# A hybrid attention and retention block on one core: the halves of retention's queries and keys exchanged by DMA

## The chip, the cores and the metric

The kernel runs on one core of a Trainium2 chip. The metric is the time of one execution in microseconds of device time, lower is better. Before the change the median of three runs is 3148.3 us (3146.62 to 3150.13).

## What is computed

One block of a streaming encoder on 4096 tokens of width 1024, in float32. Cut to what matters here:

```python
u = rms_norm(h, pre_norm_gain)
proj = einsum('bsd,de->bse', u, w_in)                 # 4104 columns
fq, fk, fv, fz, ff, rq, rk, rv, rz = split(proj)
fox = forgetting_attention(fq, fk, fv, ff + bias)     # 8 heads of 64
ret = retention(rq, rk, rv)                           # 4 heads of 128, chunkwise
out = concat([fox * silu(fz), ret * silu(rz)]) @ w_out
return h + rms_norm(out, post_norm_gain)
```

Retention rotates its queries and keys first, and this is where the change sits. The head's 128 rows are two halves of 64:

```python
def rotary(x, pos):
    x1, x2 = x[..., :64], x[..., 64:]
    return concatenate([x1 * cos - x2 * sin, x1 * sin + x2 * cos], axis=-1)
```

## The kernel before

Everything is cut into blocks of 512 tokens, eight of them. Products run on TensorE in three float16 passes. Two streams share the engines. The first is attention (`attention`): for each head and query block it takes key tiles of 128 in turn, computes scores, lets ScalarE write two exponentials, lets GpSimd subtract them (`ptt`, L308), and multiplies with the values. Beside it run the "max tiles" (`max_tile`, L999): one matmul (in the rows `ps<-kc,xq`) and one VectorE reduction (`mrow<-ps`) each, 1152 of them, which find the row maxima of later items. The second stream is the "filler": the projections of the other heads, then the output product. A credit scheme in the program decides how many filler steps are written between two attention steps, so that the order on each engine is fixed when the program is built (`tc.manual_schedule()`), and each engine works through its own list in order. PSUM has eight banks that all products take in turn; a product that needs a bank waits until the work on the bank's last contents is done.

Small follow-up work is written as Python generators. `spawn` starts one, and each `tick` (one per attention step and one per filler step) moves every live generator on to its next `yield`. So a number of `yield`s is a distance in program order, not a time.

The filler's second part, `fill_r`, projects retention's heads, two at a time (`hh` = 0 and 1), in 16 passes (two groups by eight token blocks). Per pass there are four products for queries and keys, in the order query 0, key 0, query 1, key 1. Each gives one 128 x 512 PSUM bank, and `rope_evac` takes it: ScalarE evicts it (L755), then four VectorE operations rotate it. That is 64 rotations in all. `rp` holds the cosine and sine tables of the block. All VectorE `tensor_tensor` operations go through the helper `tt`, so that their line is L141; all matmuls through `mm` (L104), all DMAs are issued by SyncE's queue through `dma` (L107), in one order.

`retention` then does one head and block: it first transposes the rotated keys on TensorE (L811), later multiplies keys with queries, updates the head's running state on VectorE (`states`, four operations `state<-state,s`), and multiplies the queries with the states. It starts at a fixed place (`pump`) while the next projection runs: for `hh` = 0 that is while the product for query 1 runs, directly behind the rotation of key 0.

Of the kernel before, what the change touches and what calls it, by code (L numbers as in the profile page):

```python
# [13 lines left out]
ALU = mybir.AluOpType  # L14
# [18 lines left out]
WAGE = 2  # L33
VAGE = 5
MAGE = 9
LEAD = 12
RAWAGE = 8
SAGE = 4
# [15 lines left out]
def kernel(  # L54
# [33 lines left out]
    def SB(tag, shape, dt=F32):  # L88
        cnt[0] += 1
        slot = SHARED.get(tag, tag)  # L90
        return sbp.tile(shape, dt, tag=slot, name=f"{tag}_{cnt[0]}", bufs=BUFS.get(slot, 1))
# [48 lines left out]
    def tt(o, a, b, op):  # L140
        nc.vector.tensor_tensor(out=o, in0=a, in1=b, op=op)  # L141

    def ts(o, a, s1, s2, op0, op1):
        nc.vector.tensor_scalar(out=o, in0=a, scalar1=s1, scalar2=s2, op0=op0, op1=op1)  # L144
# [130 lines left out]
    def iz(g, part):  # L275
        return gsc[g][part][:, KT : KT + 1]
# [477 lines left out]
    def rope_evac(p, rp, o, key):  # L754
        nc.scalar.activation(out=o, in_=p, func=AF.Copy, scale=iz(key[1], 0))  # L755
        yield 1
        yield 1
        t2 = SB("s2", [128, 512])
        tt(t2[0:64], o[64:128], rp[64:128, 1, :], ALU.mult)
        yield 1  # L760
        tt(t2[64:128], o[0:64], rp[0:64, 1, :], ALU.mult)
        yield 1
        tt(o, o, rp[:, 0, :], ALU.mult)
        yield 1
        tt(o, o, t2, ALU.add)
        done.add(key)
# [108 lines left out]
    def fill_r(G):  # L875
# [4 lines left out]
        for b, X, hook, last in group_blocks(G, tuple(range(NB))):  # L880
            vt = SB("s4", [128, 4, 256])
            zt = SB("s4", [128, 4, 256])
            for t in range(4):
                p = PS()
                for k in G.units(1, unit_N(W[1], X, t, ((0, 512),), [p])):
                    if last and t == 3 and k is not None:
                        nxt.release("wn", k)
                    yield WAIT if k is None else 3 * COST_MM + pump(k)
                spawn(evac_r(g, p, t, vt, zt))
                if t == 2:  # L890
                    rp = SB("s4", [128, 2, 512])
                    dma(rp, rope[b])
            for hh in range(2):
                qk = []
                for j in (hh, 2 + hh):
                    p = PS()
                    for k in G.units(0, unit_T(W[0], X, j * 128, p)):
                        if j == 3 and k is not None:
                            hook(k)
                            if last:  # L900
                                nxt.release("wt", k)
                        yield WAIT if k is None else 3 * COST_MM + pump(k)
                    o = SB("s2", [128, 512])
                    spawn(rope_evac(p, rp, o, ("rope", g, b, j)))
                    qk.append(o)
                rets.append(retention(b, g, hh, qk[0], qk[1], vt, zt))
                fresh[0] = rets[-1]
# [101 lines left out]
    def max_row(n, xq, mrow, qb):  # L1009
# [3 lines left out]
        ts(m4, m4, gsc[items[n][0] // 4][0][:, KT + 5 : KT + 6], None, ALU.add, ALU.bypass)  # L1013
        for _ in range(MAGE):
            yield 1
# [19 lines left out]
    def attention():  # L1035
# [52 lines left out]
        def max_rate(g):  # L1088

            rate = 0.0  # L1090
            for j in range(len(items)):
                if mdue[j] > mdone[0]:
                    if j >= 4 and first_step[j - 4] > g + 16:
                        break
                    rate = max(rate, (mdue[j] - mdone[0]) / max(first_step[j] - LEAD - g, 1))
            return min(2, math.ceil(rate - 1e-9))
# [210 lines left out]
def _constants(S):  # L1307
    import numpy as np

    half = 64  # L1310
    f = np.float32
    inv = (f(1.0) / (f(10000.0) ** (np.arange(half, dtype=f) / f(half)))).astype(f)
    ang = (np.arange(S, dtype=f)[:, None] * inv[None, :]).astype(f)
    cos = np.cos(ang.astype(np.float64)).astype(f).T
    sin = np.sin(ang.astype(np.float64)).astype(f).T
    tab = np.stack([np.concatenate([cos, cos], 0), np.concatenate([sin, -sin], 0)], 0)
    rope = np.ascontiguousarray(tab.reshape(2, 128, S // 512, 512).transpose(2, 1, 0, 3))
    lg = np.log1p(-np.exp(np.linspace(math.log(1.0 / 32), math.log(1.0 / 512), RH)))
    dk = 128.0 ** -0.5
    i = np.arange(128)  # L1320
    ii, jj = i[None, :], i[:, None]
    tri = (jj <= ii).astype(f)
    mT = np.where(jj > ii, f(NEG), f(0.0)).astype(f)
    parts = [tri, np.eye(128, dtype=f)]
    for h in range(RH):
        same = (ii // 64) == (jj // 64)
        earlier = (jj // 64) < (ii // 64)
        dist = np.where(same, np.abs(ii - jj), ii - jj)
        d = np.where(same | earlier, np.exp(lg[h] * dist), 0.0)
        parts.append((d * np.exp(-lg[h] * (ii + 1.0)) * dk).astype(f))  # L1330
    parts.append(np.stack([np.exp(lg[h] * (127.0 - i)) * dk for h in range(RH)], 1).astype(f))
    parts.append(np.stack([GN_EPS * np.exp(-2.0 * lg[h] * (i + 1.0)) for h in range(RH)], 1).astype(f))
    parts += [mT, np.ascontiguousarray(mT.T)]
    cst = np.ascontiguousarray(np.concatenate(parts, 1))
    aux = np.zeros((2 * R1 + CP + 2, 512), np.float16)
    aux[0:CP], aux[CP] = TOP, MID
    aux[2 * R1 : 2 * R1 + CP], aux[2 * R1 + CP], aux[2 * R1 + CP + 1] = TOP, MID, LOW
    return rope, cst, aux, [float(np.exp(lg[h] * 128.0)) for h in range(RH)]
# [26 lines left out]
```

## Time and profile before

| what | value |
|---|---|
| median of three runs | 3148.3 us |
| the profiled execution | 3151.84 us, its span 3150.0 us |
| mean granted TensorE clock | 0.985 |
| busy share of the span: TensorE, VectorE, ScalarE, GpSimd | 96%, 66%, 59%, 43% |
| first and last rotation (start of L755) | 1139.4 and 2704.3 us |

The profiled execution is 0.1% above the median. The span is the time from the first to the last instruction that the profiler recorded. TensorE is busy nearly throughout; its idle stretches are short and mostly end when VectorE finishes something.

### The profile page before, as it was taken

Reading aid. Unit: us, or ns where it says so; the run is one execution under the profiler, and the core shown is the slowest. Engines: PE = TensorE matmul, PEld = TensorE weight load, DVE = VectorE, ACT = ScalarE, POOL = GpSimd, SP = SyncE. Lnnn points to the kernel's source line nnn. Section 1 sums busy time; section 2 is a strip of 40 time slices with the busy share of each in tenths; the row PEclk is TensorE's granted clock in tenths of the full one; section 3 lists DMA queues with packets and bytes.
Section 4 is the critical chain, followed back from the end, with each engine's and each line's share of the span. In section 5 each row is a group of like instructions: output and inputs, shape, how many; then the busy total and the mean of one; then the engine's idle time right before and its main releaser. Section 6 shows DMA issues by size and latency. Waiting matters only on the chain.

```text
span 3150.0 us, 67744 instructions
## 1 busy us (share of the span) xinstructions
PE 3029.2 (96%) x26798; PEld 1794.7 (57%) x26799; DVE 2076.8 (66%) x4372; ACT 1873.1 (59%) x3508; POOL 1351.6 (43%) x1285
## 2 busy tenths in 40 slices
PE   8999989999999999999999999999999999889999
PEld 6666555555555555665555565556556555555554
DVE  6545567446455676777678878776877786645555
ACT  4333345676677667666667675667666766653332
POOL 0000024554555455555545564556455645540000
PEclk9999999999999999999999999999999999999999
DMA  6455753223235231311114223112111321124443
GB/s 179 156 166 152 199 123 95 67 82 93 69 88 134 64 80 35 91 51 52 55 57 101 58 71 97 51 43 78 49 51 45 111 73 33 57 68 141 141 141 120
DMA packets 266174, 284.62 MB, mean 90 GB/s; under 512 B 58976, under 2 KB 212192, under 8 KB 265856
## 3 DMA queue, kind: packets, MB, share of 16 engines
q1 hardware_dynamic: 265856, 280.30, 31.3%
q8 instruction: 210, 3.44, 0.4%
q14 instruction: 108, 0.88, 0.1%
HBM read 194.88 MB, written 88.74 MB: 90 GB/s over the span
## 4 chain that ended last, share of the span: by engine, by line
PE 80%; DVE 12%; ACT 3%; issue 2%; DMA 2%; POOL 1%; SPq 1%; POOLq 0%; DVEq 0%; ACTq 0%
PE ps L104 77%; DVE mrow L999 3%; DVE s L141 2%; DVE s L144 1%; DVE sm L141 1%; DMA rw<-in_w_in_dram 1%; ACT ph L1133 1%; PE ps L1188 1%; ACT pf L1132 1%; SPq L107 1%; PE ps L349 1%; DVE sm L144 1%; DVE s L147 1%; POOL pl L308 1%; POOL sm L308 0%
## 5 line engine op out<-in xcount | busy, mean ns | idle before, releaser
L308 POOL TENSOR_TENSOR pl<-pf,ph 128x512 f16<-128x512 f32 (+3 forms) x1152 | 1281.2, 1117 | 1135.0 <-ACT ph L1133 856.8
L1132 ACT ACTIVATE pf<-ps,gsc 128x512 f32<-128x512 f32 (+3 forms) x1152 | 758.2, 658 | 694.0 <-PE ps L104 677.0
L999 DVE TENSOR_REDUCE mrow<-ps 128x1 f32<-128x512 f32 (+3 forms) x1152 | 717.6, 641 | 356.9 <-PE ps L104 345.8
L104 PE MATMUL ps<-wn,xh 128*128 128x512 f16 (+2 forms) x3840 | 852.7, 359 | 3.1 <-DVE qk L147 2.9
L1133 ACT ACTIVATE ph<-ps,gsc 128x512 f16<-128x512 f32 (+3 forms) x1152 | 754.3, 655 | 0.0
L104 PEld LDWEIGHTS <-xh 128*128 128x128 f16 x4608 | 450.2, 98 | 450.5 <-issue 22.5
L104 PE MATMUL ps<-xh,wt 128*128 128x512 f16 x2688 | 667.7, 381 | 3.4 <-DVE mrow L999 2.0
L104 PEld LDWEIGHTS <-wt 128*128 128x128 f16 x3168 | 308.9, 98 | 356.4 <-issue 24.6
L104 PEld LDWEIGHTS <-ph 128*128 128x128 f16 x8448 | 423.9, 97 | 76.0 <-issue 8.0
L104 PE MATMUL ps<-vt,ph 128*128 128x65 f16 (+1 forms) x8448 | 433.8, 195 | 10.4 <-ACT ph L1133 7.3
L104 PE MATMUL ps<-xq,kc 99*128 99x512 f16 (+3 forms) x1152 | 420.0, 365 | 14.6 <-DMA xq<-MR 9.7
L104 PE MATMUL ps<-vt,pl 128*128 128x65 f16 x4224 | 423.4, 193 | 3.8 <-POOL pl L308 3.8
L104 PE MATMUL ps<-lq,kc 128*128 128x512 f16 (+3 forms) x1152 | 419.1, 364 | 0.0
L104 PE MATMUL ps<-kc,xq 99*128 99x512 f16 (+3 forms) x1152 | 383.1, 364 | 34.3 <-DVE mrow L999 25.1
L104 PEld LDWEIGHTS <-pl 128*128 128x128 f16 x4224 | 393.3, 99 | 5.1 <-POOL pl L308 4.7
L104 PEld LDWEIGHTS <-kc 128*128 128x128 f16 (+1 forms) x3072 | 281.9, 99 | 196.8 <-issue 22.2
L141 DVE TENSOR_TENSOR s<-s,s 64x512 f32<-64x512 f32 (+1 forms) x256 | 258.6, 1010 | 33.3 <-ACT s L755 26.3
L308 POOL TENSOR_TENSOR sm<-sm,nhalf 128x4 f32<-128x4 f32 (+2 forms) x80 | 63.0, 787 | 350.5 <-DVE sm L144 308.5
L104 PEld LDWEIGHTS <-xq 99*128 99x128 f16 x1152 | 112.3, 98 | 139.4 <-issue 9.5
L104 PE MATMUL ps<-wt,xh 128*128 128x512 f16 x768 | 184.0, 381 | 0.0
L141 DVE TENSOR_TENSOR ps<-ps,maskM 128x128 f32<-128x128 f32 x256 | 75.1, 293 | 108.4 <-PE ps L104 107.6
L141 DVE TENSOR_TENSOR xh<-ps,xh 128x256 f16<-128x256 f32 (+1 forms) x128 | 70.3, 555 | 105.5 <-ACT xh L338 86.1
(120 smaller groups left out, 2525.2 us busy)
## 6 DMA issues: line engine op xcount, KB each, us to landing
xh<-XT SPq DMA_DIRECT2D x176, 256.0 KB
rw<-in_w_in_dram SPq DMA_DIRECT2D x104, 256.0 KB
xt<-in_x_dram SPq DMA_DIRECT2D x36, 512.0 KB
s<-MX SPq DMA_DIRECT2D x32, 512.0 KB
out_dram<-xt SPq DMA_DIRECT2D x31, 512.0 KB
s<-in_x_dram SPq DMA_DIRECT2D x28, 512.0 KB
VD<-s SPq DMA_DIRECT2D x16, 516.0 KB
vt<-VD SPq DMA_DIRECT2D x64, 129.0 KB
```

What stands on the lines that cost most here:

```text
L104: nc.tensor.matmul(out=o, lhsT=lhsT, rhs=rhs, start=start, stop=stop, skip_group_check=True)
L107: nc.sync.dma_start(out=o, in_=i)
L141: nc.vector.tensor_tensor(out=o, in0=a, in1=b, op=op)
L144: nc.vector.tensor_scalar(out=o, in0=a, scalar1=s1, scalar2=s2, op0=op0, op1=op1)
L147: nc.vector.scalar_tensor_tensor(out=o, in0=a, scalar=s, in1=b, op0=op0, op1=op1)
L308: nc.gpsimd.tensor_tensor(out=o, in0=a, in1=b, op=op)
L349: nc.tensor.transpose(p[:, t * 128 : (t + 1) * 128], xs[t][:, k * 128 : (k + 1) * 128], idf)
L999: nc.vector.tensor_reduce(out=mrow[:, t, c : c + 1], in_=p[:, 0:w], axis=AX.X, op=ALU.max)
L1132: nc.scalar.activation(out=pf[:, q0:512], in_=st[:, q0:512], func=AF.Exp, scale=es)
L1133: nc.scalar.activation(out=ph[:, q0:512], in_=st[:, q0:512], func=AF.Exp, scale=es)
L1188: nc.tensor.transpose(p[:, e * 128 : (e + 1) * 128], mxt[:, half * 4 + e, :], idf)
```

## The change

The two half products with the sine table, which read one half of the rows and wrote the other, go. Two DMAs within SBUF copy the halves crosswise into `t2`; the cosine product is written directly behind them; six ticks later one VectorE operation multiplies the whole of `t2` with the sine table, and a tick later the addition follows. The sign of the sine rows in the table is exchanged to match.

```diff
+RAGE = 6
@@ rope_evac
         nc.scalar.activation(out=o, in_=p, func=AF.Copy, scale=iz(key[1], 0))
         yield 1
         yield 1
         t2 = SB("s2", [128, 512])
-        tt(t2[0:64], o[64:128], rp[64:128, 1, :], ALU.mult)
-        yield 1
-        tt(t2[64:128], o[0:64], rp[0:64, 1, :], ALU.mult)
-        yield 1
+        dma(t2[0:64], o[64:128])
+        dma(t2[64:128], o[0:64])
         tt(o, o, rp[:, 0, :], ALU.mult)
+        for _ in range(RAGE):
+            yield 1
+        tt(t2, t2, rp[:, 1, :], ALU.mult)
         yield 1
         tt(o, o, t2, ALU.add)
         done.add(key)
@@ _constants
-    tab = np.stack([np.concatenate([cos, cos], 0), np.concatenate([sin, -sin], 0)], 0)
+    tab = np.stack([np.concatenate([cos, cos], 0), np.concatenate([-sin, sin], 0)], 0)
```

The order on TensorE, ScalarE and GpSimd is the same in both programs. VectorE's list has 64 operations fewer, and SyncE's 128 DMAs more.

VectorE's list at one rotation of a key 0 (tile `s2_7243`, with `s2_7251` as `t2` and `s4_7155` as the tables; `mrow` rows are max tiles), before:

```order
L999 TENSOR_REDUCE mrow_7195_36073<-ps_7250_36346 128x1 [waits PE_49]
L141 TENSOR_TENSOR s2_7251_36349<-s2_7243_36330,s4_7155_35852 64x512 [waits Activation_49,Pool_49]
L999 TENSOR_REDUCE mrow_7195_36073<-ps_7255_36362 128x1 [waits PE_49]
L141 TENSOR_TENSOR s2_7251_36349<-s2_7243_36330,s4_7155_35852 64x512
L141 TENSOR_TENSOR s2_7243_36330<-s2_7243_36330,s4_7155_35852 128x512 [waits DMAHW3_49,DVE_49]
L999 TENSOR_REDUCE mrow_7195_36073<-ps_7261_36428 128x1 [waits PE_49]
L141 TENSOR_TENSOR s2_7243_36330<-s2_7243_36330,s2_7251_36349 128x512 [waits DVE_49]
L999 TENSOR_REDUCE mrow_7195_36073<-ps_7265_36449 128x1 [waits PE_49]
```

The same place with the change (line numbers are one or two higher):

```order
L1001 TENSOR_REDUCE mrow_7195_36121<-ps_7250_36395 128x1 [waits PE_49]
L142 TENSOR_TENSOR s2_7243_36379<-s2_7243_36379,s4_7155_35900 128x512 [waits DMAHW1_49,DMAHW0_49,DMAHW3_49,Activation_49,Pool_49]
L1001 TENSOR_REDUCE mrow_7195_36121<-ps_7255_36413 128x1 [waits PE_49]
L1001 TENSOR_REDUCE mrow_7195_36121<-ps_7261_36477 128x1 [waits PE_49]
L142 TENSOR_TENSOR s2_7251_36398<-s2_7251_36398,s4_7155_35900 128x512 [waits Pool_49]
L1001 TENSOR_REDUCE mrow_7195_36121<-ps_7265_36498 128x1 [waits PE_49]
L142 TENSOR_TENSOR s2_7243_36379<-s2_7243_36379,s2_7251_36398 128x512 [waits DVE_49]
```

The cosine product, which writes over `o`, now waits for both DMAs, which read `o`. The addition has moved from ahead of the max tile in bank tile `ps_7265` to behind it.

TensorE's list from that max tile's matmul to the transposes of this key, in both programs the same, here with the change's numbers:

```order
L105 MATMUL ps_7265_36498<-kc_6571_33181,xq_7010_35205 128x512 [waits Activation_49]
L105 LDWEIGHTS wt_5146_26195
L105 MATMUL ps_7244_36381<-xh_6997_35170,wt_5146_26195 128x512
...
L813 MATMUL ps_7266_36505<-csb_1_143,s2_7243_36379 128x128 [waits DVE_49,Activation_49]
L813 MATMUL ps_7266_36505<-csb_1_143,s2_7243_36379 128x128 x3
```

Three projection matmuls (of which one is shown) lie between the max tile and the transposes that need the rotated key. Neither has moved on TensorE; what has moved is the addition, relative to them.

VectorE's list at one rotation of a key 1 (tile `s2_5287`), where the four state updates of `hh` = 0 pass, with the change:

```order
L148 SCALAR_TENSOR_TENSOR state0_18_160<-state0_18_160,s2_5286_26919 128x128 [waits DVE_49]
L142 TENSOR_TENSOR s2_5287_26921<-s2_5287_26921,s4_5102_26002 128x512 [waits DMAHW3_49,DMAHW2_49,Activation_49]
L1001 TENSOR_REDUCE mrow_5185_26403<-ps_5304_26966 128x1 [waits PE_49]
L148 SCALAR_TENSOR_TENSOR state0_18_160<-state0_18_160,s2_5286_26919 128x128 [waits DVE_49]
L148 SCALAR_TENSOR_TENSOR state0_18_160<-state0_18_160,s2_5286_26919 128x128 [waits DVE_49]
```

Before, a half product stood where the cosine product stands now; the third and fourth state updates were behind it in either program, and are now behind an operation that waits for two DMAs.

## Rows read from the trace of the kernel before

**Rows 1.** The page: busy time by engine, and the chain that ended last.
```profile
PE 3029.2 (96%) x26798; PEld 1794.7 (57%) x26799; DVE 2076.8 (66%) x4372; ACT 1873.1 (59%) x3508; POOL 1351.6 (43%) x1285
...
PE 80%; DVE 12%; ACT 3%; issue 2%; DMA 2%; POOL 1%; SPq 1%; POOLq 0%; DVEq 0%; ACTq 0%
```

**Rows 2.** Windows: stretch; busy us and count of five engines; clock; DMA.
```profile
1135.00:2720.00 1585.00, 1517.87 (x14879) 912.70 (x14877) 1206.76 (x2356) 1072.55 (x1971) 887.53 (x788) 0.99 0.22 64
```

**Rows 3.** Groups by form: count | busy us, mean ns | idle before, releasers.
```profile
L141 DVE TENSOR_TENSOR s<-s,s 128x512 f32<-128x512 f32 x128 | 136.7, 1068 | 2.3
L141 DVE TENSOR_TENSOR s<-s,s 64x512 f32<-64x512 f32 x128 | 121.9, 952 | 31.0 <-ACT s L755 26.3 <-POOL pl L308 1.6
...
L147 DVE SCALAR_TENSOR_TENSOR state<-state,s 128x128 f32<-128x128 f32 x128 | 64.7, 506 | 11.9 <-ACT s L833 9.8
```

**Rows 4.** Timeline of SyncE, two stretches: start, us, line, DMA, count.
```profile
1656.43 0.27 SPq L107 DMA_DIRECT2D MR<-mr  x1
1658.63 0.62 SPq L107 DMA_DIRECT2D xq<-MR  x2
...
1904.28 0.35 SPq L107 DMA_DIRECT2D xq<-QX  x1
1904.73 1.10 SPq L107 DMA_DIRECT2D lq<-QX  x2
```

**Rows 5.** Timeline of ScalarE: evictions of one key 1 and three keys 0.
```profile
1149.35 0.69 ACT L755 ACTIVATE s<-ps,gsc 128x512 f32<-128x512 f32 x1
...
1783.64 0.71 ACT L755 ACTIVATE s<-ps,gsc 128x512 f32<-128x512 f32 x1
...
2368.90 0.69 ACT L755 ACTIVATE s<-ps,gsc 128x512 f32<-128x512 f32 x1
...
2679.13 0.69 ACT L755 ACTIVATE s<-ps,gsc 128x512 f32<-128x512 f32 x1
```

**Rows 6.** Timeline of VectorE beside two of these evictions.
```profile
1785.60 0.69 DVE L141 TENSOR_TENSOR s<-s,s 64x512 f32<-64x512 f32 x1
...
2369.99 0.80 DVE L141 TENSOR_TENSOR s<-s,s 64x512 f32<-64x512 f32 x1
...
2371.40 2.69 DVE L141 TENSOR_TENSOR s<-s,s 64x512 f32<-64x512 f32 x2
2374.02 0.68 DVE L999 TENSOR_REDUCE mrow<-ps 128x1 f32<-128x512 f32 x1
2374.62 1.55 DVE L141 TENSOR_TENSOR s<-s,s 128x512 f32<-128x512 f32 x1
```

**Rows 7.** Timeline of TensorE, single rows: start, us, operation, idle before and releaser.
```profile
1159.47 0.66 PE L811 MATMUL ps<-csb,s 128*128 128x128 f32 x4 [0.47 <-DVE s L141]
...
1567.71 0.39 PE L104 MATMUL ps<-kc,xq 99*128 99x512 f16 x1 [2.27 <-DVE s L141]
...
1788.13 0.49 PE L104 MATMUL ps<-state,s 128*128 128x128 f32 x2 [0.42 <-DVE state L147]
...
1906.89 1.03 PE L104 MATMUL ps<-kc,xq 99*128 99x512 f16 x2 [3.13 <-DMA lq<-QX]
...
2370.15 0.38 PE L104 MATMUL ps<-kc,xq 99*128 99x512 f16 x1
...
2375.53 0.38 PE L104 MATMUL ps<-kc,xq 99*128 99x512 f16 x1
...
2376.39 0.60 PE L811 MATMUL ps<-csb,s 128*128 128x128 f32 x4
...
2377.38 0.38 PE L104 MATMUL ps<-kc,xq 99*128 99x512 f16 x1
...
2687.17 0.60 PE L811 MATMUL ps<-csb,s 128*128 128x128 f32 x4
```

**Rows 8.** The source line L811: what its engine waited for (us, times).
```profile
  DVE s L141: 11.3, 12
```

**Rows 9.** Windows behind the wait that ended at 1567.71: columns as in rows 2.
```profile
1568.70:1571.90 3.20, 3.20 (x51) 2.77 (x49) 1.15 (x4) 0.00 (x0) 0.00 (x0) 0.50 0.56 158
```

## The prediction

> **What bounds the kernel now.** I read the page first: TensorE is busy 96% of the span and makes up 80% of the chain that ended last, VectorE 12% [rows 1]. So a change that touches VectorE and DMAs alone can move the time only through what TensorE waits for. Next the windows, for the stretch in which rotations happen: in its 1585 us TensorE is busy 1517.9, so it idles 67, VectorE is busy 1206.8 (76%) and GpSimd 887.5 (56%) [rows 2]. The reader is to see that VectorE has slack on average while TensorE has nearly none. Then the source line of the key transposes (L811): they waited for a VectorE operation of the rotation 12 times, 11.3 us in all [rows 8]. That is the place where the rotation already ends last. Last the timelines around single rotations, which give distances in time [rows 5 to 7].
>
> **What is removed.** 128 half products of 952 ns are 121.9 us of VectorE; 64 whole sine products at the mean of their kind, 1068 ns, come back as 68.4 us [rows 3]. A half product costs nearly as much as a whole one, which is where the saving of 53.5 us comes from. It is off the path: worth what waits it ends, no more. One such wait is seen: at 1567.71 TensorE had stood 2.27 us for a product that was queued behind four rotation operations, and behind it the granted clock was 0.50 (the lower level, 1.2 GHz) for 3.2 us [rows 7, 9], which costs another 1.6. With one operation fewer I count this 3.9 us as given back.
>
> **What is added: a wait.** The cosine product overwrites `o`, so it waits for both DMAs, and these for ScalarE's eviction. I call the end of the eviction E. The trace has no copy within SBUF. The nearest rows: `MR<-mr`, 2 KB out of SBUF, starts at 1656.43, and the DMA that needs it starts at 1658.63, 2.20 us later; `xq<-QX`, 99 KB into SBUF, starts at 1904.28, and TensorE goes on at 1906.89, 2.61 us later [rows 4, 7]. Two DMAs of 64 partitions take SyncE 1.10 us to issue [rows 4], so the second starts 0.55 later. The pair then lands 2.75 to 3.15 us after E; I take 2.9, between the two.
>
> VectorE got to the first half product 0.4 us after E in one place (E = 2369.59, start 2369.99) and 1.25 in another (E = 1784.35, start 1785.60) [rows 5, 6]. It will now stand 1.7 to 2.5 us at the cosine product, 64 times, some 130 us in all. Queued behind it are max tiles, and TensorE waits for their banks. In the first place the max tile whose matmul started at 2370.15 would be reduced by 2372.5 + 1.07 + 0.68 = 2374.2. Its bank is the eighth one opened afterwards, and that is the matmul at 2377.38 [rows 7]: 3.1 us to spare. So I cost this wait at nothing on TensorE, with the banks as its cover; where the cover is gone, each microsecond of it costs up to 64.
>
> The 128 issues take SyncE 64 x 1.1 = 70 us, and each pair holds the queue until its eviction is done. Behind it stand loads for later blocks and tiles, fetched ahead; I count nothing (70 if nothing were fetched ahead).
>
> On such pairs the Trainium skill has a rule that speaks against the change: "SBUF — State Buffer", section "Can I just issue two DMAs to hit both halves?", says that one DMA at partition 0 and one at partition 64 run one after the other and gain only 6%. With the fixed 2 us of its section "The DMA setup-cost knee" and the 218 GB/s that its section on the port swizzle gives for 64 partitions, two copies of 131 KB would take an estimated 2 + 2 x 0.6 = 3.2 us, and the sum below would be 5 us larger (16 x 0.3). No run here shows it yet.
>
> **What is moved.** The addition ends the rotation. It stood 5 ticks behind the eviction and stands 9 behind it now, and the transposes have not moved. In the place shown by the order it is now behind max tile `ps_7265`, three projection matmuls ahead of the transposes. Worked out there: pair landed 2372.5; cosine product to 2373.6; two reductions of 0.68 to 2374.9; sine product to 2376.0; the third reduction (its matmul, from 2375.53 for 0.38, is done by then) to 2376.7; addition to 2377.7. The transposes began at 2376.39 [rows 6, 7]: 1.3 us late.
>
> For all sixteen passes of `hh` = 0: the transposes began on average 7.4 us after E of key 0 (5.8 to 10.2; the first pair of rows gives 1159.47 - 1150.04 = 9.4, the last 2687.17 - 2679.82 = 7.4) [rows 5, 7]. Between cosine product and addition the order has 5.6 operations on average, one of them the sine product; the other 4.6, mostly max reductions and mask additions, come to 2.4 us by their own mean durations. So the addition ends at E + 2.9 + 1.07 + 1.07 + 2.4 + 1.07 = E + 8.5, on average 1.05 us late: 16 x 1.05 = 17 us. Bounds: with 2.75 for the pair and 0.69, the shortest product [rows 6], three times, it is E + 7.2, nothing lost on average; with 3.15 and 1.55, the longest shown [rows 6], E + 10.2, that is 16 x 2.8 = 45. I take the mean duration, since it holds the present mix with GpSimd.
> Two of the sixteen come out above 2 us; at the price seen above the clock costs 2 x 1.6 = 3.2.
> For `hh` = 1 the transposes come 14 us or more after E, and nothing is late.
>
> **The states.** In four of the sixteen passes the order puts a state update that TensorE needs behind the cosine product of key 1. In the one shown: E = 1784.35, landed 1787.25, cosine product to 1788.3, a reduction of 0.68 and an update of 0.51 [rows 3] to 1789.5. TensorE had started this product at 1788.13, having waited 0.42 [rows 5, 7]. So 1.4 us later, 4 x 1.4 = 5.6 (0 to 10).
>
> **Sum.** 17 + 3.2 + 5.6 - 3.9 = 21.9 us. The profiled execution would go from 3151.84 to 3174; it stood 3.5 above the median, so the median of the changed kernel comes to 3148.3 + 21.9 = 3170.
>
> **Rivals.**
> *Faster: the rotation comes in time.* VectorE has less to do, and if the addition ends before the transposes want it, the 11.3 us of waits at L811 [rows 8] and the 3.9 above go: 3148.3 - 15.2 = 3133. It decides at E + 7.4: pair and three products must take under 5.0 us together. For it speaks that a product can take 0.69 [rows 6]; against it that the mean is 1.07 and GpSimd is busy 56% of the stretch [rows 2, 3]. Chance 0.10.
> *No change.* Products of 0.85 make E + 7.85, 0.4 us late: 16 x 0.4 = 7; with 3 for the states and 3.9 given back, 6 us more, 3154. Chance 0.15.
> *Much slower: the pair takes 5 us*, because it stands in the DMA queues behind loads of 256 KB, which are issued just ahead of key 1 and between attention tiles. Each of the sixteen is then 2.1 us later, 34 us, and nearly all of them lower the clock, 14 x 1.6 = 22: 3226. Against it: the 2.61 us above were taken among other loads [rows 4]. Chance 0.10.
> That the change does not do what it says is excluded by the order: both copies and one sine product are there.
>
> **How the numbers follow.** My forecast, some 10 to 45 us more by late additions, has 0.65. What a measurement of this kernel can tell from no change is about 0.2%, 6 us. Slower by more: 0.65 + 0.10 = 0.75; within: 0.15; faster: 0.10. The range leaves out the faster rival and the upper part of the much slower one: 3143 to 3198. The forecast's own range is 3157 to 3195.
>
> **What would show it.** Right: at L811 the wait for VectorE grows from 11.3 to about 28 us or more, and its rows say that the addition released it; VectorE idles before the cosine product, released by a DMA, some 100 us or more in all; VectorE's busy time falls by some 50 us; the waits of TensorE for max reductions stay about where they were. Wrong: L811 shows no more wait than before (then the products are short, and the faster rival holds), or TensorE's waits for max reductions grow by tens of microseconds (then the banks do not cover the DMA wait), or the pair lands much earlier or later than 2.9 us behind E.

## The result and the profile after

The changed kernel takes 3221.19 us (median of 4 runs, 3219.45 to 3224.99) beside 3148.91 (4 runs, 3146.62 to 3150.13) of the kernel before: ratio 1.0228, 95% interval 1.0215 to 1.0241, 72 us slower. The direction was forecast, the size was not: 3170 was predicted, with a range of 3143 to 3198.

In the changed kernel the lines stand one or two lower: `tt` is L142, matmuls L105, DMAs L108, the rotation's eviction L756, the max reduction L1001, the transposes L813, the state update L148. First the page, its busy line, answering to [rows 1], and the copies among the DMA issues.

```profile
PE 3045.9 (95%) x26799; PEld 1798.6 (56%) x26799; DVE 2001.9 (62%) x4308; ACT 1871.3 (58%) x3508; POOL 1338.7 (42%) x1285
...
s<-s SPq DMA_DIRECT2D x128, 128.0 KB
```

VectorE's work did fall, by 75 us. Next the window over the same work as [rows 2]; its end is put 69 us later, since the last eviction of the stage is 69 us later.

```profile
1135.00:2789.00 1654.00, 1538.40 (x14873) 918.48 (x14872) 1131.66 (x2291) 1071.38 (x1970) 875.43 (x789) 0.98 0.25 71
```

The stretch grew from 1585 to 1654. TensorE idles 1654.0 - 1538.4 = 115.6 in place of 67.1, so 48.5 more; and for the same matmuls (14873 and 14879) it is busy 1538.4 in place of 1517.9, 20.5 more. The second part is the clock, by which TensorE works at full speed (1.0 in the rows, 2.4 GHz) or at the lower level (0.5, 1.2 GHz). The mean granted clock of each whole run, the kernel before and the changed one:

```profile
core 0: 3150.0 us, clock 0.985
```
```profile
core 0: 3217.7 us, clock 0.980
```

Within the two stretches the trace's record of the granted clock has TensorE at the lower level for 41.0 us before and 81.9 after; 41 us more at half speed cost 20.5 us, which is what the busy time grew by.

Then what TensorE waited for (total us, times, longest), the kernel before and the changed one:

```profile
PE ps L104 <- DVE mrow L999: 34.5, 37, 4.2
PE ps L104 <- DVE state L147: 7.4, 9, 2.9
PE ps L811 <- DVE s L141: 4.3, 4, 2.6
```
```profile
PE ps L105 <- DVE mrow L1001: 43.5, 35, 4.2
PE ps L813 <- DVE s L142: 33.4, 16, 3.6
PE ps L105 <- DVE state L148: 18.6, 11, 5.1
```

The differences are 29.1 at the transposes, 11.2 at the states and 9.0 at the max reductions; their sum, 49.3, is near the 48.5 of idle time. So three waits and the clock hold the loss in this stage. The source line L813, answering to [rows 8], and VectorE's products and its wait for the copies, answering to [rows 3]:

```profile
  DVE s L142: 52.7, 23
  issue: 18.4, 7
```
```profile
L142 DVE TENSOR_TENSOR s<-s,s 128x512 f32<-128x512 f32 x192 | 186.1, 970 | 167.0 <-DMA s<-s 134.7 <-ACT pf L1134 15.7 <-POOL pl L309 7.1
```

The source line counts weight loads with the matmuls, so its 52.7 holds most waits twice; the row of TensorE above does not.

One rotation of a key 0 shows the first wait. The four timelines are those of ScalarE, SyncE, VectorE and TensorE of the changed kernel.

```profile
2106.31 0.69 ACT L756 ACTIVATE s<-ps,gsc 128x512 f32<-128x512 f32 x1
```
```profile
2107.06 1.11 SPq L108 DMA_DIRECT2D s<-s  x2
```
```profile
2110.05 0.75 DVE L142 TENSOR_TENSOR s<-s,s 128x512 f32<-128x512 f32 x1 [3.99 <-DMA s<-s]
2110.72 1.87 DVE L1001 TENSOR_REDUCE mrow<-ps 128x1 f32<-128x512 f32 x3
2112.52 2.26 DVE L142 TENSOR_TENSOR s<-s,s 128x512 f32<-128x512 f32 x2
```
```profile
2114.92 1.09 PE L813 MATMUL ps<-csb,s 128*128 128x128 f32 x4 [3.08 <-DVE s L142]
```

The eviction ends at 2107.00. The copies are issued at once, and the cosine product starts 3.05 us later. Three reductions, two of them held back behind it, come in one bunch; only then the sine product and the addition, which ends at 2114.78. TensorE stood ready 3.08 us earlier. A window behind it:

```profile
2115.00:2117.00 2.00, 2.00 (x26) 1.94 (x27) 0.00 (x0) 0.00 (x0) 0.00 (x0) 0.50 0.00 0
```

TensorE is busy throughout, at the lower level. Nine of the sixteen waits at the transposes are over 2 us, by its timeline, and a tenth is 1.99. The clock fell in or behind five of the nine only. A window behind the wait of 2.78 that ended at 2217.80, where it stayed up:

```profile
2217.90:2219.90 2.00, 2.00 (x20) 1.27 (x21) 0.69 (x1) 0.97 (x2) 0.00 (x0) 1.00 0.03 8
```

One rotation of a key 1 shows the second wait: SyncE, VectorE and TensorE.

```profile
1695.02 1.41 SPq L108 DMA_DIRECT2D rw<-in_w_in_dram  x3
1696.54 1.11 SPq L108 DMA_DIRECT2D s<-s  x2
```
```profile
1702.44 0.69 DVE L142 TENSOR_TENSOR s<-s,s 128x512 f32<-128x512 f32 x1 [5.79 <-DMA s<-s]
1703.05 0.29 DVE L142 TENSOR_TENSOR ps<-ps,maskM 128x128 f32<-128x128 f32 x1
1703.37 0.42 DVE L1001 TENSOR_REDUCE mrow<-ps 128x1 f32<-128x256 f32 x1
1703.71 0.61 DVE L148 SCALAR_TENSOR_TENSOR state<-state,s 128x128 f32<-128x128 f32 x2
```
```profile
1704.05 0.80 PE L105 MATMUL ps<-state,s 128*128 128x128 f32 x2 [5.07 <-DVE state L148]
```

The eviction had ended at 1695.88. Three weight loads of 256 KB stood ahead in SyncE's queue: the copies went out 0.66 us late, and their data came 5.8 us after that. For all of this time VectorE stood at a product that nobody needed yet, with a state update behind it that TensorE did.

### The profile page after: what moved, and what is told of

It reads as the page before. It is cut to its first block, busy times and chain, and to the rows that moved or that the text cites. A ratio compares the mean times of both kernels' runs of the same rounds, so it can differ in the third digit from the quotient of the medians.

```text
span 3217.7 us, 67945 instructions
## 1 busy us (share of the span) xinstructions
PE 3045.9 (95%) x26799; PEld 1798.6 (56%) x26799; DVE 2001.9 (62%) x4308; ACT 1871.3 (58%) x3508; POOL 1338.7 (42%) x1285
## 5 line engine op out<-in xcount | busy, mean ns | idle before, releaser
L309 POOL TENSOR_TENSOR pl<-pf,ph 128x512 f16<-128x512 f32 (+3 forms) x1152 | 1268.3, 1105 | 1207.0 <-ACT ph L1135 928.9
L1001 DVE TENSOR_REDUCE mrow<-ps 128x1 f32<-128x512 f32 (+3 forms) x1152 | 717.5, 641 | 365.7 <-PE ps L105 354.7
L105 PE MATMUL ps<-wn,xh 128*128 128x512 f16 (+2 forms) x3840 | 856.5, 360 | 3.8 <-DVE qk L148 3.6
L105 PEld LDWEIGHTS <-xh 128*128 128x128 f16 x4608 | 451.0, 98 | 452.7 <-issue 27.1
L105 PE MATMUL ps<-xh,wt 128*128 128x512 f16 x2688 | 673.2, 383 | 3.2 <-DVE mrow L1001 1.8
L105 PEld LDWEIGHTS <-wt 128*128 128x128 f16 x3168 | 310.0, 98 | 357.7 <-issue 28.6
L105 PEld LDWEIGHTS <-ph 128*128 128x128 f16 x8448 | 425.9, 97 | 75.8 <-issue 8.3
L105 PE MATMUL ps<-xq,kc 99*128 99x512 f16 (+3 forms) x1152 | 422.2, 367 | 29.9 <-DVE mrow L1001 19.2
L105 PE MATMUL ps<-vt,ph 128*128 128x65 f16 (+1 forms) x8448 | 435.7, 195 | 10.9 <-ACT ph L1135 7.3
L105 PE MATMUL ps<-vt,pl 128*128 128x65 f16 x4224 | 425.0, 193 | 4.4 <-POOL pl L309 4.3
L105 PE MATMUL ps<-lq,kc 128*128 128x512 f16 (+3 forms) x1152 | 421.3, 366 | 0.0
L105 PE MATMUL ps<-kc,xq 99*128 99x512 f16 (+3 forms) x1152 | 384.2, 365 | 27.5 <-DVE mrow L1001 19.4
L105 PEld LDWEIGHTS <-kc 128*128 128x128 f16 (+1 forms) x3072 | 281.5, 98 | 213.5 <-issue 41.4
L105 PEld LDWEIGHTS <-pl 128*128 128x128 f16 x4224 | 394.3, 100 | 5.6 <-POOL pl L309 5.4
L142 DVE TENSOR_TENSOR s<-s,s 128x512 f32<-128x512 f32 x192 | 186.1, 970 | 167.0 <-DMA s<-s 134.7
L105 PEld LDWEIGHTS <-xq 99*128 99x128 f16 x1152 | 112.8, 99 | 138.4 <-issue 10.7
L105 PE MATMUL ps<-wt,xh 128*128 128x512 f16 x768 | 183.1, 380 | 0.0
L142 DVE TENSOR_TENSOR ps<-ps,maskM 128x128 f32<-128x128 f32 x256 | 75.1, 293 | 113.2 <-PE ps L105 112.6
L142 DVE TENSOR_TENSOR xh<-ps,xh 128x256 f16<-128x256 f32 (+1 forms) x128 | 70.2, 556 | 104.3 <-ACT xh L339 84.6
```

What stands on the lines that cost most here:

```text
L105: nc.tensor.matmul(out=o, lhsT=lhsT, rhs=rhs, start=start, stop=stop, skip_group_check=True)
L309: nc.gpsimd.tensor_tensor(out=o, in0=a, in1=b, op=op)
L1001: nc.vector.tensor_reduce(out=mrow[:, t, c : c + 1], in_=p[:, 0:w], axis=AX.X, op=ALU.max)
```

## Experiments

A first set separates the two costs that the changed order brings: that VectorE waits for the copies (because the cosine product overwrites what they read), and that the addition stands late. Each can be had without the other. The changed kernel and the three with the early addition, with a tile of its own, and with both are all the combinations; two more are the kernel before with lateness alone.

**The changed kernel, addition early.**
```
-RAGE = 6
+RAGE = 2
```


> Of the changed kernel only the distance is changed: 2 ticks instead of 6 between cosine and sine product, so that the addition stands 5 ticks behind the eviction as it did before; the DMAs and VectorE's wait for them at the cosine product stay. Theory A, the late addition (it ends the key 0 rotations some 2 us after the transposes want them, TensorE waits, and the clock falls behind each such wait): most of the loss of 72 us goes, 3150 to 3170, the waits for VectorE at the key transposes fall from 53 us to below 25. Theory B, VectorE's wait for the DMAs: 3205 to 3220, and the transposes wait as long as in the changed kernel, since the wait alone delays the rotation.

Measured: 3184.31 us (3181.41 to 3185.51), ratio 1.0110 [1.0095, 1.0125]; 37 us came back. Its waits of TensorE:

```profile
PE ps L105 <- DVE mrow L1001: 38.3, 35, 4.2
PE ps L105 <- DVE state L148: 18.2, 10, 5.0
PE ps L105 <- DVE s L142: 5.7, 4, 2.0
PE ps L813 <- DVE s L142: 5.2, 6, 2.6
```

The time lies between the two ranges. The wait at the transposes is nearly gone, that at the states stays whole. So lateness is not all.

**The kernel before, only the addition four ticks later, no copies.**
```
         yield 1
+        for _ in range(4):
+            yield 1
         tt(o, o, t2, ALU.add)
```


> The kernel before with its four VectorE operations and no DMA, only that the addition stands four ticks later, as in the changed kernel. Theory A: the addition alone costs much of the 72 us, 3180 to 3215, with 35 us or more of waits for VectorE at the key transposes. Theory B: 3145 to 3155, no loss without the DMAs.

Measured: 3168.05 (3166.61 to 3175.67) beside 3150.87, ratio 1.0065 [1.0044, 1.0086]: plus 17, between the two ranges.

**The changed kernel, cosine product into a tile of its own.** The product then overwrites nothing that the copies read, so VectorE doesn't wait there.
```
+        oc = SB("s2", [128, 512])
-        tt(o, o, rp[:, 0, :], ALU.mult)
+        tt(oc, o, rp[:, 0, :], ALU.mult)
-        tt(o, o, t2, ALU.add)
+        tt(o, oc, t2, ALU.add)
```


> The changed kernel with the cosine product into a tile of its own, so that it doesn't overwrite what the DMAs read and doesn't wait for them; the addition stays 9 ticks behind the eviction. Theory A: hardly better, 3195 to 3220. Theory B: the loss goes, 3145 to 3160. In both the 135 us of VectorE's waits for the copies nearly vanish.

Measured: 3186.72 (3182.23 to 3189.40), ratio 1.0118 [1.0102, 1.0133], again between the two ranges. VectorE's wait for copies fell from 134.7 to 11.9 us; the states' wait of TensorE went back to 6.2, that at the transposes only to 25.5.

**Both: own tile, addition early.** The diffs of the first and the third together.

> Both edits: the cosine product into its own tile and 2 ticks to the sine product, so that VectorE waits for the copies at the sine product only. Theory A: 3145 to 3165, about as the kernel with the early addition alone. Theory B: as the one with the own tile alone, 3145 to 3165, or slower by what the sine product still waits. If the two causes add up, only this one comes back to the kernel before, and the two single edits each keep 20 to 50 us of the loss.

Measured: 3140.26 (3133.27 to 3142.65), ratio 0.9966 [0.9954, 0.9978]: with the copies the kernel is 10.6 us faster than before. That is below both ranges, and the last sentence of the expectation holds: each single edit keeps 33 to 36 us of the loss. Window over its stage, in which TensorE idles 52.4 us (58.4 in the kernel before, from 1140 to 2705), then its waits of TensorE:

```profile
1140.00:2694.00 1554.00, 1501.64 (x14781) 903.12 (x14780) 1118.52 (x2266) 1059.94 (x1949) 871.65 (x780) 0.99 0.26 74
```
```profile
PE ps L105 <- DVE mrow L1002: 35.7, 33, 4.2
...
PE ps L105 <- DVE state L148: 5.2, 7, 1.7
```

So the copies themselves, their traffic and their 128 issues cost nothing that shows. From this kernel, VectorE's wait alone costs 3184.3 - 3140.3 = 44 us, lateness alone 3186.7 - 3140.3 = 46, and both 81, nearly the sum. In the traces, over the stage, the 44 are about 32 us of idle time and 9 of longer busy time, the 46 about 31 and 17.

**The kernel before with two operations late, no copies.** The addition alone late cost 17, but 46 in the set above. The changed order puts a product late as well; here the cosine product takes that place.
```
-        yield 1
         tt(t2[64:128], o[0:64], rp[0:64, 1, :], ALU.mult)
-        yield 1
+        for _ in range(6):
+            yield 1
         tt(o, o, rp[:, 0, :], ALU.mult)
```


> The kernel before, without any copy: both half products come early, where the change issues its copies, and the cosine product (in place) and the addition stand late, where the change has its sine product and addition. VectorE waits for no DMA. If it is the late place alone that costs (two operations of 1.07 us instead of one behind the late tick, so each addition about a microsecond later than in the kernel with only the addition late, which lost 17 us), the time is before plus 35 to 50, 3183 to 3198, as in the changed kernel with its own tile for the cosine product (plus 36 to 38). If the copies add something there (their late landings, the sine product waiting for them), it stays near before plus 17 to 25, 3165 to 3173.

Measured: 3196.27 (3193.06 to 3200.04) beside 3150.09, ratio 1.0146 [1.0133, 1.0160]: plus 46, as much as lateness costs with the copies. TensorE's waits:

```profile
PE ps L104 <- DVE mrow L999: 42.1, 38, 4.2
PE ps L811 <- DVE s L141: 29.4, 15, 3.9
PE ps L104 <- DVE state L147: 11.9, 11, 3.5
```

So lateness costs this much without any DMA.

**Where VectorE's wait is paid.** Two kernels with the addition early divide the own tile: only key 1 has it, or all but key 1.
```
+        oc = SB("s2", [128, 512]) if key[3] == 3 else o
```


> Addition early (2 ticks), and only the rotation of key 1, one in four, has the cosine product in its own tile; the other three still wait for the copies at the cosine product. Theory S (VectorE's wait at the copies is paid by the state updates queued behind it in the rotation of key 1): most of the 44 us between 3184 and 3140 goes, 3145 to 3160, and TensorE's waits at the states fall from 18 us to about 7. Theory M (it is paid everywhere, by max tiles and evictions): a quarter goes, 3168 to 3178.

> The complement: own tile for query 0, key 0 and query 1, only key 1 waits for the copies at the cosine product. Theory S: 3160 to 3180, with some 18 us of waits at the states. Theory M: 3146 to 3155.

Measured beside 3147.46: 3157.41 (3154.27 to 3163.27), ratio 1.0033 [1.0022, 1.0044], and 3162.29 (3159.45 to 3164.24), ratio 1.0046 [1.0029, 1.0063]. Against the kernel before, the wait at all four rotations stands at +33.4, without key 1 at +9.9, at key 1 alone at +14.8, and nowhere at -10.6. So key 1, a quarter of the rotations, makes 23 to 25 of the 44. Of the last kernel two waits:

```profile
PE ps L105 <- DVE mrow L1002: 34.2, 30, 4.2
PE ps L105 <- DVE state L148: 18.9, 11, 5.2
```

All the states' wait is there, and the max reductions wait no more than before. Of the other three rotations' 20 us no single wait was isolated: with key 1 spared, TensorE's waits that name a rotation's operation on VectorE (at transposes and other matmuls) come to 10.3 us, against 2.4 with the own tile everywhere.

**The transposes later instead.** Retention of `hh` = 0 starts one slot of `pump` later, in the changed kernel and in the one before.
```
+    late = [0]
+        if not evac[0] and rets[0] is fresh[0] and late[0] > 0:
+            late[0] -= 1
+            return 0
+                late[0] = 1 - hh
```


> The changed kernel, in which retention of the first head of a pair starts one slot later, four projection steps on: its key transposes come behind the late addition. Theory A for one half of the loss (the late addition is paid at the transposes): the waits for VectorE there fall from 53 us to under 10 and the time to 3160 to 3185. Rival (the late addition is paid by everything behind it on VectorE, not at the transposes): 3205 to 3220.

> The kernel before with the same later start. The 11.3 us of waits at the transposes go; if nothing else moves, 3135 to 3142. Rival: the later start shifts the four state updates onto other work, and the time stays at 3145 to 3160.

Measured beside 3147.46: 3160.54 (3153.59 to 3162.26), ratio 1.0038 [1.0022, 1.0054], and 3153.06 (3147.06 to 3154.84), ratio 1.0011 [1.0001, 1.0020]. One slot gives the changed kernel 59 of its 72 us back, and the kernel before nothing (it is 5.6 us slower); there TensorE's waits for max reductions grow instead (34.5 to 39.1 at the same matmuls). It moves the state updates with the transposes and mends both waits: of 18.6 us for the states 5.5 are left, and the transposes wait no more for a rotation.

**Can the fast version be made faster?** Own tile and early addition, with the later use, and with 3 ticks before the sine product in place of 2.

> The changed kernel with its own tile for the cosine product, the addition early (2 ticks) and the retention of key hh = 0 one slot later. If TensorE still loses at the transposes, the later use gains a few microseconds on the 3140 of the version without it: 3130 to 3137. If the waits there are already gone (1.1 us were left) and the later use only pushes max tiles together, as in the kernel before with the later use (plus 4), it is 3140 to 3146.

> The changed kernel with its own tile for the cosine product and the sine product 3 ticks behind it instead of 2. In the version with 2 ticks VectorE still stood 47.7 us at the sine product for the copies, 35 times. With 3 that should fall to 20 to 30 us. If such waits of VectorE still cost TensorE anything, the time falls below 3140, by up to 6 us: 3134 to 3140. If the tick's delay of the addition costs more (a quarter of the 46 us that four ticks cost, 11 us, or less while the addition is still in time), 3140 to 3152.

Measured beside 3150.09: 3151.25 (3145.58 to 3154.56), ratio 1.0004 [0.9995, 1.0013], and 3143.62 (3137.98 to 3148.59), ratio 0.9977 [0.9968, 0.9987]. The later use takes the gain away, beyond both of its ranges. With 3 ticks VectorE's wait for copies fell from 47.7 to 27.0 us, and the time did not fall: the interval overlaps that with 2 ticks. Whether what VectorE still waits there costs anything is not shown: with 3 ticks the addition stands later, too, and the two may cancel.

## Why the prediction was wrong

**The late addition: right mechanism, mis-sized term.** "So the addition ends at E + 2.9 + 1.07 + 1.07 + 2.4 + 1.07 = E + 8.5, on average 1.05 us late: 16 x 1.05 = 17 us." Over the sixteen passes of the trace after, the addition ended on average at E + 9.2, 1.8 us behind the 7.4; TensorE waited 33.4 us at the transposes, 2.1 each, 29.1 more than before. In that trace the missing 0.7 us stands ahead of the cosine product: it started at E + 3.6 on average, not at E + 2.9, and in five of the sixteen behind E + 4. The three products took 3.0 us together in place of 3.2, what lies between them 2.6 in place of 2.4. Yet that late start is not what the lateness needs: with the cosine product in its own tile, which takes VectorE's wait away, the addition still ended at E + 8.8, and with no copy at all and two operations late at E + 9.0, with 29.4 us of wait. What the sum lacked is TensorE's own order. It gave the reductions their busy time (2.4 us), but a reduction also waits for its matmul, and the late products stand behind it. One pass shows it on VectorE, first in the changed kernel (E = 1460.55), then in the kernel before with two operations late (E = 1456.23):

```profile
1466.23 0.69 DVE L1001 TENSOR_REDUCE mrow<-ps 128x1 f32<-128x512 f32 x1 [0.61 <-PE ps L105]
1466.84 2.47 DVE L142 TENSOR_TENSOR s<-s,s 128x512 f32<-128x512 f32 x2
```
```profile
1461.92 0.69 DVE L999 TENSOR_REDUCE mrow<-ps 128x1 f32<-128x512 f32 x1 [0.30 <-PE ps L104]
1462.52 2.48 DVE L141 TENSOR_TENSOR s<-s,s 128x512 f32<-128x512 f32 x2
```

In both the two late operations start 6.29 us behind E, with the copies and without. Between the early products and the addition VectorE waited for TensorE in five of the sixteen passes of the changed kernel, and in eleven where no copy held it up.

**The clock: mis-sized term, and the largest miss.** "Two of the sixteen come out above 2 us; at the price seen above the clock costs 2 x 1.6 = 3.2." Nine of them were above 2 us, and so were three of the states' waits; in the whole stage 23 waits of TensorE were, and 10 before. The busy time grew by 20.5. But the clock did not fall at every such wait, as the first expectation above has it. In the two stretches it fell 8 times before and 19 times after: at 1 and 5 of the waits at the transposes, at 1 and 2 of the states', at 3 and 10 of those for max reductions, and at three and two others. So the count was wrong, and only in part by the first term: seven of the eleven more falls belong to waits for max reductions, which the sum had at nothing. Why 10 of their 10 waits over 2 us lowered the clock after the change, and 3 of 6 before, stays open. One fall more cost 1.9 us, near the 1.6.

**The states: right place, mis-sized term.** "So 1.4 us later, 4 x 1.4 = 5.6 (0 to 10)." At the place worked out, TensorE waited 1.62 after and 0.42 before, 1.2 more. But three others waited 5.07, 4.03 and 2.79, and the total grew by 11.2. In the two longest of these waits the copies landed 5.6 and 6.4 us after E, behind weight loads. "The pair takes 5 us" was a rival for all rotations; it holds for five of the 64 pairs, two of key 1, two of key 0 and one of query 1. That its 3226 lies near the 3221 measured is luck. With the clock behind them and the other rotations, VectorE's wait costs 44 us, as the set of four shows.

**"So I cost this wait at nothing on TensorE, with the banks as its cover": wrong as a whole, right for the banks.** With VectorE's wait and the addition early, max reductions cost TensorE 38.3 us, against 35.7 with the own tile. The cover holds. But the step looked at max tiles alone as what is queued behind the wait; the state updates and rotations, which no bank covers, stood in the same queue. The 9.0 us of more max waits in the changed kernel go with lateness: 42.1 without a copy.

**Given back: more than counted, but only where nothing else was lost.** "With one operation fewer I count this 3.9 us as given back." The set shows -10.6 with both costs taken away. VectorE's busy time fell by 75, not 53.5, mostly because the products took 970 ns on average and not 1068. The wait of 2.27 at that place is gone in the trace after, too. The rival "faster", which the own tile and the early addition in effect bring about, gave 3133; measured 3140. It counted the 11.3 us of [rows 8] as gone, and so misread them: that row counts weight loads with the matmuls, and TensorE's matmuls waited only 4.3 us there, 4 times.

**The sum, as measured.** In the trace the terms come to 29.1 + 20.5 + 11.2 + 9.0 = 69.8, where the forecast had 17 + 3.2 + 5.6 + 0, less 3.9. By the set of four, -10.6 + 44 + 46 is 80 us; together the two costs overlap by 9 or 10, which leaves 70 against the kernel before as measured beside that set (3150.87; the 72 stand against 3148.91).

**The pair: right on a free queue, short as a mean.** 2.9 us were taken; where SyncE's queue was free the product started about 3.05 behind E, with the copies' landing about 0.1 ahead of it, and the median of the 64 pairs is 3.0. The mean is 3.5, and 3.4 for the sixteen pairs of key 0, which the sum needed: some were issued late or landed among loads. The estimate made from the Trainium skill ("SBUF — State Buffer", "Can I just issue two DMAs to hit both halves?") was 3.2, a little long for a free queue; whether the two copies run one after the other, no run here shows. Its rule would not have mended the forecast either: 5 us more were 45 too few.

**No cost of the issues:** 128 more DMAs on SyncE were counted at nothing, and with the own tile and the early addition nothing is seen of them.

What stays open: which waits make up the 20 us that the three rotations other than key 1 cost, and how much of the overlap is the same wait counted twice.

## What to carry to other kernels

A DMA that reads a tile makes the next in-place operation on that tile wait for it, and all that is queued behind on that engine; look there for the operation with no slack, not for the most frequent one, and give the in-place operation a tile of its own. When an operation gets a fixed distance to wait out a DMA, look at what the operation is moved behind: its distance in time is not the busy time of the work ahead of it, but also what that work waits for on another engine. Here both mends together turned a change that loses 2.3% into one that gains 0.3%, while either alone left it 1.1% to 1.2% slower.

## What was not expected of the hardware

Of the 46 pairs of copies that were issued within 0.1 us of their source, 33 landed 2.85 to 3.02 us behind it and the others up to 4.5; two pairs directly behind three 256-KB loads landed 5.6 and 6.4 us behind it, although their issue was only 0.7 to 0.9 us late. The granted clock falls already in the wait and not only behind it: 0.82 on average in 3.4 us of the wait that ended at 1704.05. Windows inside that wait and behind it, to the return of the full clock, and then behind the wait of 3.08 us that ended at 2114.92:

```profile
1699.00:1702.40 3.40, 0.00 (x0) 0.00 (x0) 0.00 (x0) 0.00 (x0) 0.47 (x1) 0.82 0.62 160
```
```profile
1707.00:1708.00 1.00, 1.00 (x23) 1.00 (x21) 0.00 (x0) 0.00 (x0) 0.68 (x1) 0.50 0.07 16
1708.00:1709.00 1.00, 1.00 (x15) 0.73 (x13) 0.11 (x1) 0.26 (x1) 0.00 (x0) 1.00 0.00 0
```
```profile
2117.00:2117.60 0.60, 0.60 (x15) 0.60 (x13) 0.00 (x0) 0.00 (x0) 0.00 (x0) 0.50 0.00 0
2117.60:2118.20 0.60, 0.60 (x20) 0.58 (x18) 0.00 (x0) 0.00 (x0) 0.00 (x0) 0.99 0.00 0
```

TensorE worked at the lower level for about 4.0 us behind the wait of 5.07, and for 2.7 behind that of 3.08.
